# One step of a hybrid decoder layer on one core: 1 / rms of the input made during the second FFN pair, low parts of weights a step behind their casts, SSM sums a sample behind updates

## The chip, the cores and the metric

The kernel runs on one core of one Trainium2 chip. A core has a matrix engine (TensorE, PE in the profile, with its weight loads as PEld), three engines for elementwise work (VectorE = DVE, ScalarE = ACT, GpSimd = POOL) and SyncE (SP), which issues the DMAs. Each engine takes its own instructions in order; semaphores join them. The metric is the device time of one execution in microseconds (us), the median over the runs.

## The reference, cut to what matters

T = 1048 tokens (16 meta, 1024 of a prompt, 8 samples of one token each) go through one layer in f32, D = 1024, D_FF = 2816:

```python
def rmsnorm(x, w):
    y = x * lax.rsqrt(jnp.mean(x * x, axis=-1, keepdims=True) + EPS)
    return y * w

def swiglu(x, wg, wu, wd):
    return (jax.nn.silu(x @ wg) * (x @ wu)) @ wd

h += 0.5 * swiglu(rmsnorm(h))               # FFN 1
u  = rmsnorm(h) @ w_in                      # q, f, v, g of 4 HGRN2 heads; z, x, B, C, dt of Mamba-2
...                                         # HGRN2: f = lb + (1 - lb) sigmoid(u_f), k = 1 - f, q = silu(u_q)
...                                         # Mamba-2: conv + silu, chunked scan; per sample:
                                            #   state = exp(dt A) state + dt x B^T, y = state C + D x
h += concat(hgrn_out, ssm_out) @ w_out      # ssm_out = grouped rmsnorm(y * silu(z))
h += 0.5 * swiglu(rmsnorm(h))               # FFN 2
```

Outputs are the normed h and the states of both recurrences.

## The kernel before, in words

**Products.** A number in f32 is split into a high part, rounded to the type that TensorE multiplies (`CAST` on ACT), and a low part, the rest (a subtraction on DVE). A product takes three matmuls (`mm3`, L143 to L145: high × high, high × low, low × high).

**The FFN's pairs.** Gate and up projections of one block f of 128 columns (22 in all) are a *pair*. It is computed as a two by two block product in seven products (numbered 1 to 7) over two halves of the tokens: 14 *steps* of 12 matmuls. Each step's operands are blocks or sums of blocks: on the side of the tokens (class `Blocks`, named `o` and `e` in `first1` for the two halves, L287 sums, L292 high, L298 low parts, each 128 × 1048), on the side of the weights (class `Left`: loads, L360 sums, L364 high, L368 low parts, 128 × 512). After a step `post` adds the product into the results on DVE (`L452`, `L457`, `L462` and so on) or copies it on ACT (L450), multiplies by 1 / rms of the tokens (`times_r`, L445; the norm's weight is in the input blocks already) and applies silu. Two such pairs make the input of one block pair of the down projection (`Hidden.jobs`), which comes in its own 7 products.

**Order.** In both FFNs the order on PE, DVE, ACT and SP is written by hand: `S.add` appends a step, `S.before(i, fn)` puts work ahead of step i, and `Steps.run` issues all of it, on each engine in that order. In the middle of the kernel (projections, scans, output projection) a scheduler orders the instructions by the code and its own estimates.

**The head of FFN 1** (`first1`, classes `Input` and `Blocks`). x is loaded in ten tiles of 128 tokens and transposed on TensorE (`place`, L843; `place_k`, L868). Tiles 0 to 4 are the half `o`, tiles 5 to 9 the half `e`. Each transposed block is written scaled by the norm's weight (L855, L870) and raw (L859, L871; the raw blocks go to memory by `store`, to be added to h later). The sum of squares of each token is an ACT instruction per tile (`square`, L887). `rms(half)` makes 1 / rms of five tiles and writes it on the diagonal of identity tiles (L902), `spread_r(half)` multiplies these by ones so that each partition has the row (L908), and copies it (L909). In the first pair this was made for the half `o` ahead of step 5 and for `e` ahead of step 10, between the pair's own steps; the first pair's steps take the tokens half by half, the later pairs' by turns.

**The SSM scan.** `ssm_scan` takes nine chunks of 128 tokens: L1111 makes decays from running sums loaded from memory (`cumd`), L1112 an Exp, L1114 products on DVE, which TensorE needs at L1118; L1125 and L1129 update the state that TensorE needs in the next chunk (L1104). `ssm_samples` gives nine jobs, one for each of the 8 samples and one at the end, which are handed out in `hgrn_project` of the first head while the scan runs: a sample's state and B, C rows are loaded into two of the eight `r` buffers, POOL updates the state (L1191, L1195, L1196, per group g of heads), DVE sums it against C (four instructions, L1198), and SP stores it.

**The projections of HGRN2 head 0** (`hgrn_project`): for q a Silu (ACT) of each of three chunks of tokens, for f two Sigmoids (one for f and one for k = 1 − f), between the Exps of the scan. ACT loads a table (`ACT_TABLE_LOAD`) when the function changes.

**The second norm of Mamba-2** (`ssm_norm(K, 1, "u")`, L1232 to L1242): squares on ACT, a sum on POOL (L1233), three matmuls with ones (L1237), then a multiplication on DVE. After it comes `out_proj`.

Of the kernel before, what the change touches and what calls it, by code (L numbers as in the profile page):

```python
# [17 lines left out]
P = 128  # L18
# [5 lines left out]
NS = 8  # L24
# [318 lines left out]
class Left:  # L343
# [30 lines left out]
    def plan(self, S, s0, late):  # L374
# [52 lines left out]
def pair(K, S, wg, wu, f, ops, spread, hid, first=None):  # L427
# [20 lines left out]
    def post(p, cs, b):  # L448
        if p == 1:
            nc.scalar.copy(temp("z", cs), b)  # L450
        elif p == 6:
            nc.vector.tensor_add(temp("v", cs), b, temp("z", cs))  # L452
        elif p == 2:
# [4 lines left out]
        elif p == 7:  # L458
            nc.vector.tensor_add(temp("u1", cs), b, temp("x", cs))
            times_r("u1", 1, cs)  # L460
        elif p == 3:
            nc.vector.tensor_add(temp("g1", cs), b, temp("v", cs))  # L462
            t = times_r("g1", 1, cs)
            nc.scalar.activation(t, t, AF.Silu)  # L464
        else:
            nc.vector.tensor_add(temp("u0", cs), b, temp("v", cs))
            times_r("u0", 0, cs)
            if "h" not in tm:
                tm["h"] = True
                hid.append(K.slot("s", T))  # L470
            for n in range(2):
                nc.vector.tensor_mul(halves(hid[0][:, n * 2 * Q : n * 2 * Q + 2 * Q])[:, cs], temp(f"g{n}", cs), temp(f"u{n}", cs))

    if not first:
        left.plan(S, s0, int(f == 1))
# [5 lines left out]
    def post_first(p, cs, b):  # L481

        if p in (5, 2):
            late[p] = b
        elif p == 7:
            nc.vector.tensor_add(temp("u1", cs), b, temp("x", cs))
        elif p == 3:
            post(2, cs, late[2])
            post(3, cs, b)
            times_r("u1", 1, cs)  # L490
# [187 lines left out]
def ffn(K, wg, wu, wd, ops, spread, src, first, after):  # L678
# [9 lines left out]
    with K.tc.manual_schedule(engines={E.PE, E.DVE, E.Activation, E.SP}):  # L688
        S = Steps()
        hidden = Hidden(K)  # L690
        for i in range(NF // 2):
            hid, e = [], []
            for f in (2 * i, 2 * i + 1):
                hid.append([])
                pair(K, S, wgv, wuv, f, ops, spread, hid[-1], first if f == 0 else None)
                e.append(len(S.steps))
            hidden.jobs(S, i, hid, *e)
# [110 lines left out]
class Input:  # L808
# [3 lines left out]
    def __init__(self, K, a, wcol, ops, spread):  # L812
# [3 lines left out]
        self.x, self.diag = {}, {}  # L816
# [72 lines left out]
    def store(self, half):  # L889
        dv = self.d.rearrange("(b k p) t -> b p k t", p=P, b=2)  # L890
        for q in (2 * half, 2 * half + 1):
            for b in range(2):
                self.K.nc.sync.dma_start(dv[b][:, :, q * Q : q * Q + Q], self.raw[b, q])

    def rms(self, half):

        K = self.K
        token_rstd(K, *(self.st[:, j, 5 * half : 5 * half + 5] for j in range(3)))
        d = self.diag[half] = K.t(2 * Q)
        for i in range(5):  # L900
            c = slice(P * i, min(P * i + P, 2 * Q))
# [956 lines left out]
```

## Time and profile before

| | us |
|---|---|
| median of 3 runs | 2137.22 (2134.08 to 2138.86) |
| profiled execution, its own time | 2141.21 |
| its span | 2139.4 |
| TensorE busy | 2021.8 (95%) |
| VectorE busy | 1491.7 (70%) |
| ScalarE busy | 803.0 (38%) |
| GpSimd busy | 141.3 (7%) |

The span runs from the first to the last instruction of the profiled execution; 1.8 us of its time lie around it. FFN 1 begins at once and its pairs last until about 490 us, the scan is between 880 and 980, the second FFN's pairs lie between 1440 and 1860. A busy TensorE isn't always at its peak: the granted clock (PEclk) says at what share of full speed it ran. An engine's idle time matters only where TensorE waits for it. In rows of a timeline the columns are start, duration, engine, line, operation, output<-inputs, shape, count, and in brackets the idle time before and what ended it; DVE's sums of the samples stand there as CUSTOM_DVE_ANT_0, in the order below as ISA.

### The profile page before, as it was taken

Reading aid. Unit: us, or ns where it says so; the run is one execution under the profiler, and the core shown is the slowest. Engines: PE = TensorE matmul, PEld = TensorE weight load, DVE = VectorE, ACT = ScalarE, POOL = GpSimd, SP = SyncE. Lnnn points to the kernel's source line nnn. Section 1 sums busy time; section 2 is a strip of 40 time slices with the busy share of each in tenths; the row PEclk is TensorE's granted clock in tenths of the full one; section 3 lists DMA queues with packets and bytes.
Section 4 is the critical chain, followed back from the end, with each engine's and each line's share of the span. In section 5 each row is a group of like instructions: output and inputs, shape, how many; then the busy total and the mean of one; then the engine's idle time right before and its main releaser. Section 6 shows DMA issues by size and latency. Waiting matters only on the chain.

```text
span 2139.4 us, 38417 instructions
## 1 busy us (share of the span) xinstructions
PE 2021.8 (95%) x15495; PEld 1965.4 (92%) x15495; DVE 1491.7 (70%) x2489; ACT 803.0 (38%) x1494; POOL 141.3 (7%) x175
## 2 busy tenths in 40 slices
PE   5999999999899899799999998979999999989996
PEld 5999999999899889788989997979999999989996
DVE  6777777777787676596454366677777777778863
ACT  7422222223335443562432335652222222324342
POOL 1000000000002110321111010220000000000000
PEclk8999999999999999999999999999999999999999
DMA  6323333246956511452022053313233242587651
GB/s 189 89 81 100 103 93 105 78 131 228 295 165 194 155 47 31 119 154 75 32 71 79 2 176 107 103 60 106 88 107 105 76 120 81 172 265 230 208 166 59
DMA packets 325033, 259.17 MB, mean 121 GB/s; under 512 B 17712, under 2 KB 301104, under 8 KB 324848
## 3 DMA queue, kind: packets, MB, share of 16 engines
q1 hardware_dynamic: 324616, 256.68, 39.5%
q8 instruction: 122, 2.00, 0.4%
q14 instruction: 55, 0.45, 0.1%
q0 software_dynamic: 224, 0.04, 0.0%
q10 hardware_dynamic: 16, 0.00, 0.0%
HBM read 191.26 MB, written 65.47 MB: 120 GB/s over the span
## 4 chain that ended last, share of the span: by engine, by line
PE 78%; DVE 8%; DMA 6%; ACT 3%; issue 2%; SPq 1%; POOL 1%; DVEq 0%; ACTq 0%; POOLq 0%
PE acc L143 24%; PE acc L144 23%; PE acc L145 23%; DMA r<-in_w_ffn_down_dram 2%; DMA r<-in_w_ffn_up_dram 2%; PE mis L1355 2%; DMA u<-hd 1%; DVE s L634 1%; DVE u L287 1%; DVE r L360 1%; PE mis L1394 0%; PE mis L1450 0%; DVE ws L616 0%; DVE u L298 0%; PE mis L1412 0%
## 5 line engine op out<-in xcount | busy, mean ns | idle before, releaser
L143 PE MATMUL acc<-u,ws 128*128 128x262 f32 (+2 forms) x4504 | 1326.9, 296 | 56.5 <-DVE s L634 20.1
L144 PE MATMUL acc<-u,ws 128*128 128x262 f32 (+2 forms) x4504 | 1315.6, 292 | 0.6 <-DVE u L563 0.3
L145 PE MATMUL acc<-u,ws 128*128 128x262 f32 (+2 forms) x4504 | 1313.9, 292 | 1.0 <-DVE ws L368 0.8
L143 PEld LDWEIGHTS acc<-u,ws 128*128 128x128 f32 x4504 | 858.2, 191 | 75.1 <-issue 21.7
L144 PEld LDWEIGHTS acc<-u,ws 128*128 128x128 f32 x4504 | 862.4, 191 | 2.5 <-DVE u L563 0.7
L145 PEld LDWEIGHTS acc<-u,ws 128*128 128x128 f32 x4504 | 858.3, 191 | 1.9 <-DVE ws L368 1.0
L368 DVE TENSOR_TENSOR ws<-r,ws 128x512 fp32r<-128x512 f32 x308 | 212.0, 688 | 103.7 <-ACT ws L364 103.7
L364 ACT CAST ws<-r 128x512 fp32r<-128x512 f32 x308 | 173.3, 615 | 4.7 <-PE acc L145 3.1
L464 ACT ACTIVATE t<-t 128x524 f32<-128x524 f32 (+1 forms) x46 | 28.6, 622 | 313.1 <-DVE t L445 313.1
L360 DVE TENSOR_TENSOR r<-r,r 128x512 f32<-128x512 f32 x176 | 119.1, 697 | 19.0 <-DMA r<-in_w_ffn_up_dram 17.0
L634 DVE SCALAR_TENSOR_TENSOR s<-acc,s 128x524 f32<-128x524 f32 (+1 forms) x120 | 77.6, 663 | 48.8 <-PE acc L145 47.6
L455 ACT ACTIVATE t<-t 128x524 f32<-128x524 f32 (+1 forms) x46 | 28.7, 623 | 216.7 <-DVE t L445 216.7
L204 POOL TENSOR_TENSOR t<-t,t 128x262 f32<-128x262 f32 x56 | 52.9, 960 | 813.2 <-ACT t L203 813.2
L563 DVE TENSOR_TENSOR u<-u,u 128x1048 fp32r<-128x1048 f32 (+1 forms) x84 | 97.1, 1159 | 8.8 <-ACT u L559 8.8
L445 DVE TENSOR_TENSOR t<-t,u 128x524 f32<-128x524 f32 (+1 forms) x138 | 93.6, 681 | 4.7
L138 DVE TENSOR_TENSOR ws<-r,ws 128x512 fp32r<-128x512 f32 x88 | 60.2, 698 | 39.2 <-ACT ws L137 39.0
L611 ACT CAST ws<-r 128x512 fp32r<-128x512 f32 (+1 forms) x84 | 47.8, 581 | 102.9 <-DVE r L606 39.3
L616 DVE TENSOR_TENSOR ws<-r,ws 128x512 fp32r<-128x512 f32 (+1 forms) x84 | 57.2, 691 | 41.6 <-ACT ws L611 41.5
L611 ACT CAST ws<-u 128x512 fp32r<-128x512 f32 (+1 forms) x72 | 42.1, 585 | 113.2 <-DVE u L606 110.9
L559 ACT CAST u<-u 128x1048 fp32r<-128x1048 f32 (+1 forms) x84 | 83.2, 992 | 2.0 <-DMA u<-hd 2.0
L137 ACT CAST ws<-r 128x512 fp32r<-128x512 f32 x88 | 53.8, 617 | 71.7 <-PE acc L145 51.9
L445 DVE TENSOR_TENSOR t<-acc,u 128x524 f32<-128x524 f32 (+1 forms) x46 | 31.3, 680 | 61.6 <-PE acc L145 61.6
(379 smaller groups left out, 1950.1 us busy)
## 6 DMA issues: line engine op xcount, KB each, us to landing
hd<-s SPq DMA_DIRECT2D x170, 262.0 KB
r<-in_w_ffn_down_dram SPq DMA_DIRECT2D x128, 256.0 KB
u<-hd SPq DMA_DIRECT2D x56, 524.0 KB
r<-in_w_ffn_gate_dram SPq DMA_DIRECT2D x88, 256.0 KB
r<-in_w_ffn_up_dram SPq DMA_DIRECT2D x88, 256.0 KB
r<-in_w_in_dram SPq DMA_DIRECT2D x56, 256.0 KB
r<-in_w_ffn_down_dram SPq DMA_DIRECT2D x64, 192.0 KB
u<-hd SPq DMA_DIRECT2D x28, 393.0 KB
```

The source lines that it names most:

```text
L138: self.nc.vector.tensor_sub(lo, src, hi.bitcast(F32))
L143: mm(ps, whi, xhi, start=first, stop=False, skip_group_check=more)
L144: mm(ps, whi, xlo, start=False, stop=False, skip_group_check=more)
L145: mm(ps, wlo, xhi, start=False, stop=last, skip_group_check=more)
L360: self.K.nc.vector.tensor_tensor(self.raw[p], self.raw[x], self.raw[y], op)
L364: self.K.nc.scalar.copy(self.w[p][:, : self.n * P], self.raw[p])
L368: self.K.nc.vector.tensor_sub(t[:, 512 : 512 + w], self.raw[p], t[:, :w].bitcast(F32))
L445: nc.vector.tensor_mul(t, t if src is None else src, spread.lanes(i, cs))
L559: K.nc.scalar.copy(hi, lo.bitcast(F32))
L563: K.nc.vector.tensor_sub(lo, lo.bitcast(F32), hi.bitcast(F32))
L611: nc.scalar.copy(w[p, j, g][:, : n * P], src)
L634: nc.vector.scalar_tensor_tensor(t, b, 0.5, t, ALU.mult, ALU.add)
```

## The change

1. *The head.* All ten squares come later (two of the smaller tiles at steps 1 and 4, the others ahead of steps 9 to 16), `rms` is made once for all ten columns ahead of step 18, its diagonal is one buffer of full width, and the four spread matmuls stand ahead of step 22, in the second pair. The first pair's results stay unscaled until then: six jobs ahead of steps 26 to 31 do its scaling, silu and products. `post` of product 2 is an ACT copy in the first two pairs. The jobs of the first block pair of the down projection wait for that (steps 32 and 33), and the second pair's weight sums come four steps later. The first pair's other preparations are spread anew over steps 1 to 11.
2. *Weights.* In all pairs of both FFNs the loads come one step earlier, and the low part (L368) one step behind its cast. `times_r("u1")` goes from the post of product 7 to that of product 3.
3. *The samples.* Job b updates sample b on POOL and then sums sample b − 1 on DVE and stores it: ten jobs, four in place of three for each projection of head 0.
4. *Head 0's q and f.* ACT copies the chunks raw; Silu or the Sigmoids run once over all tokens, behind the third chunk.
5. *The second norm's end* (matmuls and multiplication) is written behind the first quarter of `out_proj`.

```diff
 class Left.plan
-            ((1, 7, 4, 2), (-10, -10, -9, -9), self.load),
-            ((5, 6, 7, 3), (-7, -7, -6, -5), self.sum_),
-            (ORDER, [2 * i - 4 + late for i in range(7)], self.split),
+            ((1, 7, 4, 2), (-11, -11, -10, -10), self.load),
+            ((5, 6, 7, 3), [d + sums for d in (-7, -7, -6, -5)], self.sum_),
+            (ORDER, [2 * i - 4 + late for i in range(7)], self.hi),
+            (ORDER, [2 * i - 3 + late for i in range(7)], self.lo),
 pair, post
+        elif p == 2 and late_r and f < 2:
+            nc.scalar.copy(temp("g0", cs), b)
 ...
         elif p == 7:
             nc.vector.tensor_add(temp("u1", cs), b, temp("x", cs))
-            times_r("u1", 1, cs)
         elif p == 3:
             nc.vector.tensor_add(temp("g1", cs), b, temp("v", cs))
-            t = times_r("g1", 1, cs)
-            nc.scalar.activation(t, t, AF.Silu)
+            if late_r and f == 0:
+                return
+            if late_r and f == 1:
+                silu(0, cs)
+            silu(1, cs)
+            times_r("u1", 1, cs)
 ...
+    if late_r:
+        cs = slice(0, 2)
+        for i, (fn, *args) in enumerate(((silu, 0, cs), (silu, 1, cs), (times_r, "u0", 0, cs), (product_, 0, cs), (times_r, "u1", 1, cs), (product_, 1, cs))):
+            S.before(s0 + late_r + i, lambda fn=fn, args=args: fn(*args))
 first1
-        before(S, 4, (o.low, 3), (w.lo, 3), (tail,), (e.cast, 1), (e.sum_, 5), (o.cast, 4), (x.place_k, 4), (x.rms, 0), (x.place_k, 5))
-        before(S, 5, (x.spread_r, 0), (o.low, 4), (e.cast, 5), (e.low, 1), (x.place_k, 6), (x.place_k, 7), (x.store, 1))
 ...
+        for i, n in enumerate((3, 5, 6, 7, 8)):
+            before(S, 12 + i, (x.square, n))
+        before(S, 18, (x.rms,))
+        before(S, 22, *((x.spread_r, q) for q in range(4)))
 ssm_samples
-            for j in (2 * g, 2 * g + 1):
-                nc.vector.tensor_tensor_reduce(up[:, j % 2], sb[:, j], rows[:, 2 + g], 1.0, 0.0, ALU.mult, ALU.add, ys[:, j, b : b + 1])
+    def sample(b):
+        if b < NS:
+            update(b)
+        if b > 0:
+            output(b - 1)
 hgrn_project
+            nc.scalar.copy(out[x][:, c0 : c0 + w], ps)
+            left[0] -= 1
+            if left[0] == 0:
+                (ev_q if x == "q" else ev_f)(0, T, out[x])
 out_proj
+        if u == 1 and mid:
+            mid()
```

What this does to the order of instructions at three places. First ACT in the head, from the cast of token block 5 on. Before (u and ws are operands of tokens and weights, L859 raw copies, L887 a square, L450 the copy of the first product):

```order
L292 CAST u_244<-u_241 128x1048
L364 CAST ws_248<-r_246 128x512
L859 COPY u_202<-mis_226 128x4x12
L859 COPY u_205<-mis_226 128x4x12
L887 ACTIVATE s_115,st_103<-s_115 128x1024
L450 COPY t_275<-acc_262 128x262
L292 CAST u_280<-u_259 128x1048
```

and now (L452 is the copy of the first product, L877 the raw copies, L888 and L889 a placement of the half e, L905 a square of a small tile):

```order
L452 COPY t_257<-acc_244 128x262
L292 CAST u_259<-u_242 128x1048
L364 CAST ws_263<-r_261 128x512
L877 COPY u_202<-mis_226 128x4x12
L877 COPY u_205<-mis_226 128x4x12
L905 ACTIVATE u_126,st_103<-u_126 12x1024
L888 ACTIVATE u_282<-mis_277,col_100 128x262
L889 COPY u_284<-mis_277 128x262
```

The cast of block 5 now stands behind the copy of the first product, the first placement of e ahead of the second step, and the square of a full tile is gone from here.

Second DVE in the scan, at the fourth chunk. Before (L1114 the chunk's products, L1198 the sums of sample 3, whose state is r_10418, L1125 what the scan goes on with):

```order
L1114 TENSOR_TENSOR s_9710<-s_9710,s_9712 128x512 x2
L1198 ISA t_10423,s_9643<-r_10418,r_10419 128x128
L1198 ISA s_9643 128x1
L1198 ISA t_10423,s_9643<-r_10418,r_10419 128x128
L1198 ISA s_9643 128x1
L1198 ISA t_10428,s_9643<-r_10418,r_10419 128x128
L1198 ISA s_9643 128x1
L1198 ISA t_10428,s_9643<-r_10418,r_10419 128x128
L1198 ISA s_9643 128x1
L1125 TENSOR_TENSOR s_9712<-mis_9751,s_9712 128x512
```

and now (L1130 and L1141 are those lines, L1221 the sums, of sample 2, whose state is r_10288):

```order
L1130 TENSOR_TENSOR s_9697<-s_9697,s_9699 128x512 x2
L1221 ISA t_10316,s_9630<-r_10288,r_10289 128x128
L1221 ISA s_9630 128x1
L1221 ISA t_10316,s_9630<-r_10288,r_10289 128x128
L1221 ISA s_9630 128x1
L1221 ISA t_10316,s_9630<-r_10288,r_10289 128x128
L1221 ISA s_9630 128x1
L1221 ISA t_10316,s_9630<-r_10288,r_10289 128x128
L1221 ISA s_9630 128x1
L1141 TENSOR_TENSOR s_9699<-mis_9738,s_9699 128x512
```

As many sums stand between the two lines, but those of the sample before.

Third PE at the second norm. Before (L1237 the norm's matmuls, L143 to L145 the projections; acc_13185 is the last of the gate's in its first rows, then the first of `out_proj`):

```order
L145 MATMUL acc_13185<-u_8294,ws_13045 128x348
L1237 MATMUL mis_13266<-u_13261,ones_83 128x350
L1237 MATMUL mis_13269<-u_13261,ones_83 128x350
L1237 MATMUL mis_13272<-u_13261,ones_83 128x348
L143 MATMUL acc_13185<-u_8287,ws_13303 128x262
```

and now (L1270 for L1237):

```order
L145 MATMUL acc_13176<-u_8281,ws_13036 128x348
L1270 MATMUL mis_13337<-u_13252,ones_83 128x350
L143 MATMUL acc_13176<-u_8274,ws_13275 128x262
L1270 MATMUL mis_13340<-u_13252,ones_83 128x350
L1270 MATMUL mis_13343<-u_13252,ones_83 128x348
L144 MATMUL acc_13176<-u_8282,ws_13275 128x262
```

The scheduler has put the norm's first matmul ahead of the projection still, and one matmul of it between.

More of the change, by code (lines that the diff above doesn't have):

```diff
@@ L694, in ffn @@
                 hid.append([])
-                pair(K, S, wgv, wuv, f, ops, spread, hid[-1], first if f == 0 else None)
+                pair(K, S, wgv, wuv, f, ops, spread, hid[-1], first if f == 0 else None, late_r)
                 e.append(len(S.steps))
-            hidden.jobs(S, i, hid, *e)
+            hidden.jobs(S, i, hid, *([late_r + 6, late_r + 7] if late_r and i == 0 else e))
         h = []
@@ L1614, in first1 @@
         o.low(2)
+        w.lo(2)
         o.sum_(5)
[L1616 to L1625 removed]
         def tail():
```

127 lines of the change are left out of this document (69 added, 58 removed).

## The prediction

> **What bounds the kernel now.** I read the page first (busy time, slices, chain), then TensorE's waits, and then windows and single instructions where TensorE isn't full.
>
> ```profile
> span 2139.4 us, 38417 instructions
> PE 2021.8 (95%) x15495; PEld 1965.4 (92%) x15495; DVE 1491.7 (70%) x2489; ACT 803.0 (38%) x1494; POOL 141.3 (7%) x175
> PE   5999999999899899799999998979999999989996
> PE 78%; DVE 8%; DMA 6%; ACT 3%; issue 2%; SPq 1%; POOL 1%; DVEq 0%; ACTq 0%; POOLq 0%
> ```
>
> TensorE bounds it, 95% busy, and the chain of waits is 78% TensorE. No edit removes matmuls in number, so the change can only win where TensorE stands still or runs at a low clock: the first slice, and the slices around 900 us. The first 100 us in four windows (columns: length, busy time and count of each engine, granted clock, DMA share, GB/s):
>
> ```profile
> core 0: us, PE busy (x) PEld busy (x) DVE busy (x) ACT busy (x) POOL busy (x), PEclk, DMA share, GB/s
> 25.00:50.00 25.00, 17.98 (x104) 16.26 (x102) 14.54 (x27) 22.78 (x58) 0.00 (x0) 0.75 0.23 63
> 50.00:75.00 25.00, 18.12 (x108) 17.46 (x108) 21.61 (x39) 18.95 (x35) 0.00 (x0) 0.80 0.25 74
> 75.00:100.00 25.00, 25.00 (x207) 25.00 (x206) 18.57 (x31) 7.13 (x13) 0.00 (x0) 1.00 0.31 94
> ```
>
> From 75 us on TensorE is full: 207 matmuls in 25 us, 0.121 us each, so a step of the pair (12 matmuls) takes 1.45 us. Before that it does 104 and 108, at clocks of 0.75 and 0.80.
>
> **Part 1, the head of FFN 1: −7.5 us.** The first pair's 14 steps, as TensorE saw them:
>
> ```profile
> 21.97 0.58 PE L143 MATMUL acc<-u,ws 128*128 128x262 f32 x1 [4.13 <-ACT t L450]
> 42.78 2.12 PE L908 MATMUL mis<-t,ones 128*128 128x262 f32 x4 [4.81 <-ACT t L902]
> 55.19 0.59 PE L143 MATMUL acc<-u,ws 128*128 128x262 f32 x1 [5.12 <-ACT t L450]
> 64.33 1.73 PE L908 MATMUL mis<-t,ones 128*128 128x262 f32 x4 [1.75 <-ACT t L902]
> 72.75 0.28 PE L143 MATMUL acc<-u,ws 128*128 128x262 f32 x1
> ```
>
> The second step (step 1) starts at 21.97, the second pair at 72.75: 50.8 us for 13 steps, which at 1.45 would take 18.9. That leaves 32 us, of which the spread of 1 / rms shows 4.81 + 1.75 of waiting and 2.12 + 1.73 of slow matmuls. What ACT and DVE have to make for these steps is priced by these groups (0 to 75 us; columns: busy us, mean ns, idle before):
>
> ```profile
> L292 ACT CAST u<-u 128x1048 fp32r<-128x1048 f32 x14 | 14.8, 1068 | 2.1 <-DVE u L287 2.1
> L887 ACT ACTIVATE s<-s 128x1024 f32<-128x1024 f32 x8 | 8.6, 1078 | 0.0
> L870 ACT ACTIVATE u<-mis,col 128x262 f32<-128x262 f32 (+1 forms) x16 | 8.1, 506 | 0.0
> L871 ACT COPY u<-mis 128x262 f32<-128x262 f32 (+1 forms) x16 | 6.4, 399 | 0.0
> L298 DVE TENSOR_TENSOR u<-u,u 128x1048 fp32r<-128x1048 f32 x14 | 17.2, 1243 | 0.4 <-ACT u L292 0.4
> L287 DVE TENSOR_TENSOR u<-u,u 128x1048 f32<-128x1048 f32 x8 | 10.0, 1244 | 0.0
> L368 DVE TENSOR_TENSOR ws<-r,ws 128x512 fp32r<-128x512 f32 x9 | 6.2, 685 | 0.0
> L360 DVE TENSOR_TENSOR r<-r,r 128x512 f32<-128x512 f32 x8 | 5.4, 686 | 0.0
> ```
>
> Moved off the first pair's way: 8 squares (8.6 us of ACT), the 10 pieces of the diagonal, the spread and its waits, the scaling and silu. What must still be made there: on DVE 12 low parts at 1.24, 8 sums at 1.24, 9 weight pieces at 0.69, with eight adds of the products at 0.43 (estimate, half of a full-width add): 14.9 + 9.9 + 6.2 + 3.4 = 34.5 us; on ACT 12 casts at 1.07, 16 + 16 placements at 0.51 and 0.40, and some 5 of weight casts and copies: 12.8 + 14.5 + 5 = 32.3. Both begin near 18 us, so the last step can't begin before about 52: at most 20 us can come back. The beginning can't be earlier either:
>
> ```profile
> GB/s 0 61 135 292 297 284 371 338 348 329 203 282 321 362 404 406 422 387 355 346 336 277 331 328 200 222 229 200 73 3 0 0 0 0 0 154 342 49 0 0
> 12.29 1.06 PE L843 MATMUL mis<-ident,s 128*128 128x128 f32 x8 [1.22 <-DMA s<-in_x_prompt_dram]
> 18.00:20.00 2.00, 0.00 (x0) 0.00 (x0) 2.00 (x5) 1.28 (x2) 0.00 (x0) 0.50 1.06 351
> 22.00:24.00 2.00, 2.00 (x9) 2.00 (x10) 2.00 (x4) 1.44 (x3) 0.00 (x0) 0.50 1.04 330
> ```
>
> Summing the first row (1 us slices), the tile that TensorE takes at 12.29 was through at about 9.7 us, and all of x with the weights between (5.29 MB) is through at 18.1. With the same lag the last tile is usable at 20.5, and step 1 now stands behind its first placement: about 21.4 against 21.97, no gain. From there I walked ACT and DVE through the new order, an instruction starting when its engine and its inputs are free (each hand-off costs what the row gives): step 1 ends at 24.1, steps 3, 5 and 7 at 30.1, 38.3 and about 50.2, the last two low parts are written at 57.4 and 59.6, and the last step ends near 61.7. Against 72.75 that is −11. From it goes back: the four spread matmuls now lie in the full second pair (in before 2.12 + 1.73 = 3.85, half of that at full clock, +1.9, nothing else covers them), and the first pair's scaling, silu and products land in steps 25 to 38, where DVE gets some 31 instructions of about 0.65 in 14 steps of 1.45: 20.2 against 20.3 us, no slack, so +1.6 for two or three of them that come late (2.5 × 0.65). Sum −7.5; from −3 (the walk's hand-offs hold at half of its gain) to −11.
>
> The trace shows 18 to 20 at a clock of 0.50, and 22 to 24 too (9 matmuls in 2.00, 0.22 each), behind a wait of 4.13; in the new order TensorE stands from 21.97 − 4.13 = 17.84 to the placement at 20.5, 2.7. The Trainium skill, TensorE: Matmul & The Clock Gate, section HAM oscillation, has the clock drop after some 3.4 us of idleness. By that rule 12 matmuls after 2.7 would keep the full clock, an estimated 1.2 us less; no row here shows a wait of 2.7, and I leave it out.
>
> **Part 2, low parts a step behind, loads a step earlier, one scaling moved: −1 us.** What stands there, in the full pairs of FFN 1 (75 to 490 us; columns: total, times, longest):
>
> ```profile
> PE acc L143 <- DVE t L457: 1.4, 4, 0.5
> DVE ws L368 <- ACT ws L364: 49.0, 41, 1.2
> ```
>
> DVE waits 49 us for casts, but TensorE only 1.4 in all for it: DVE's idleness costs nothing, so 1.4 in each FFN is the most to be had, and a low part written later can cost as much where DVE is late: −1, from −2 to +1.5.
>
> **Part 3, the SSM scan, sums a sample behind updates, Silu and Sigmoid late: −7 us.** Two waits of TensorE, and the windows around them:
>
> ```profile
> PE mis L1118 <- DVE s L1114: 7.6, 2, 6.2
> PE mis L1104 <- DVE s L1125: 5.6, 2, 5.2
> 892.42 2.44 ACT L1111 ACTIVATE s<-s,s 128x128 f32<-128x128 f32 x8 [3.92 <-DMA s<-cumd]
> 894.88 1.28 ACT L1121 ACT_TABLE_LOAD   x1
> 898.60:904.80 6.20, 6.18 (x32) 5.25 (x32) 0.48 (x1) 6.08 (x11) 1.38 (x2) 0.53 0.99 268
> 904.80:910.00 5.20, 0.09 (x1) 0.00 (x0) 3.67 (x9) 0.00 (x0) 5.20 (x9) 0.80 0.27 75
> 910.00:915.00 5.00, 4.91 (x20) 4.91 (x20) 5.00 (x13) 3.30 (x6) 1.75 (x3) 0.53 0.55 124
> 906.33 0.80 DVE L1198 CUSTOM_DVE_ANT_0 t<-r,r 128x128 f32<-128x128 f32 x1 [7.26 <-POOL r L1196]
> ```
>
> The second wait (5.2) is an order on DVE: what the scan waits for (L1125) is queued behind the sums of sample 3, and these wait 7.26 for POOL. In the new order sample 2's stand there, whose update ended earlier, so the 5.2 goes, with the slow clock after it: 910 to 915 runs at 0.53, half of 4.6 us is 2.1. The first wait (6.2) is for cumd, whose load stays behind a store on SP; only the table load of 1.28 goes, since the raw copies leave Exp's table in place. 5.2 + 2.1 + 1.3 = 8.6. Against it: SP's load of sample 6 waits for a buffer freed behind chunk 3, with chunk 4's cumd queued behind it, which nothing covers; I take off a fifth for it, 1.6, and at worst all 8.6 goes back. −7, from 0 to −12 (two more of the waits behind POOL gone).
>
> **Part 4, the end of the second norm put behind the first projection: 0.**
>
> ```profile
> PE mis L1237 <- POOL u L1233: 4.7, 1, 4.7
> ```
>
> In TensorE's new order the first of the norm's three matmuls still stands ahead of the projection's first, and one matmul of that between it and the others, so the 4.7 stays (at best −0.1; at worst +0.5, if the multiplications by the norm come late).
>
> **Sum.** −7.5 − 1 − 7 = −15.5. The profiled execution took 2141.21 (span 2139.4 and 1.8 around it), 3.99 above the median of the runs: 2125.7 for it, 2121.7 for the median; I say 2122.
>
> **The rivals.**
> *The head is bound by hand-offs and not by work* (14%). For: DVE was busy 14.54 of 25 and still late. Then the walk's gain shrinks to 3.5, which the spread and the jam mostly take: −2 instead of −7.5, 2127.
> *The scan waits elsewhere* (13%). For: the loads on SP. Its second wait then becomes one of cumd, −0 for −7: 2129.
> *More than I count* (12%): the head −11, the scan −12, the pairs −2: 2112.
> *Nothing gained* (9%): both of the first two together leave −2 − 1 − 0 = −3, 2134; with the pairs' +1.5 in place of −1 about 2137.
> *Slower* (6%): sums beside updates. The prices of one sum, and of L1129 beside POOL and later:
>
> ```profile
> L1198 DVE CUSTOM_DVE_ANT_0 t<-r,r x32: 277/286/1134, 886.9 to 946.6; 128x128 f32<-128x128 f32 x32
> L1198 DVE CUSTOM_DVE_ANT_0 t<-r,r 128x128 f32<-128x128 f32 x32 | 14.5, 501 | 9.1 <-POOL r L1196 9.1
> 922.37 2.96 DVE L1129 SCALAR_TENSOR_TENSOR u<-u,s,s 128x128 f32<-128x128 f32 x4
> 933.08 1.13 DVE L1129 SCALAR_TENSOR_TENSOR u<-u,s,s 128x128 f32<-128x128 f32 x4
> ```
>
> A sum takes 0.28 alone and 0.80 to 1.13 beside POOL (shortest, median and longest in the first row). At a mean of 0.50 (second row) some 8 of 32 lie beside it now: 24 × 0.28 + 8 × 1.13 = 15.8, about the 14.5 there. If the 24 others come to lie beside the next sample's update too, that is 24 × 0.85 = 20.4, and four chunks' L1129 at 2.96 for 1.13 add 7.3: 27.7 us of DVE within the scan. If TensorE waits for all of it, the scan is 27.7 − 8.6 = +19.1, the total −7.5 − 1 + 19.1 = +10.6, 2148. It decides where the surplus exceeds 8.6 + 8.5 = 17 us; against it, DVE did nothing in most of 898.60 to 904.80 (0.48 of 6.20), so there is slack. The Trainium skill, SBUF — State Buffer, section Who interferes with whom, says that a VectorE instruction with two SBUF inputs and a GpSimd one that reads SBUF block each other wholly; the 0.80 beside the 0.28 agrees in direction.
>
> **How the numbers follow.** The forecast has 46%. A measurement of this kernel tells about 0.2% (4.3 us) from no change. Faster by more than that: forecast, both half-failures, the larger gain: 85%. Within: 9%. Slower: 6%. The range leaves out the last two and the far end of the larger gain: 2111 (head −11, pairs −2, scan −12, less 1) to 2133 (half of the head alone).
>
> **What would show it.** Right: the second pair starts near 63 us in place of 72.75; no wait at L1104 of 5 us near 905; the wait at the second norm stays near 4.7; 75 to 490 unchanged within 2 us but for some 3 lost in the second pair. Wrong: the second pair at 70 or later; sums (L1221 after) of 0.8 or more with TensorE waiting behind them; more than 5 us of waits between 65 and 90.

## The result and the profile after

The changed kernel takes 2120.10 us, median of 5 runs (2118.52 to 2124.35), against 2138.86 for the kernel before (5 runs, 2134.08 to 2144.28): ratio 0.9915, 95% interval 0.9895 to 0.9934, so 18 us less (14 to 22). The forecast was 2122, 15.5 less. The profiled execution took 2120.27, its span is 2118.6; that of before was 2139.4.

The head of FFN 1, in the windows of 25 us that were shown of before (same columns):

```profile
25.00:50.00 25.00, 15.67 (x100) 13.59 (x99) 18.60 (x23) 18.49 (x44) 0.00 (x0) 0.87 0.46 135
50.00:75.00 25.00, 23.38 (x177) 22.28 (x177) 17.55 (x31) 20.84 (x45) 0.00 (x0) 0.99 0.15 43
```

From 50 to 75 us TensorE does 177 matmuls instead of 108. From 25 to 50 it does no more than before; it stands for 9 us there (7 before), but the granted clock is 0.87 (0.75 before). TensorE's timeline at the points that the forecast named:

```profile
20.20 0.57 PE L143 MATMUL acc<-u,ws 128*128 128x262 f32 x1
45.06 0.59 PE L143 MATMUL acc<-u,ws 128*128 128x262 f32 x1 [3.57 <-ACT u L292]
60.47 0.29 PE L143 MATMUL acc<-u,ws 128*128 128x262 f32 x1
72.64 1.93 PE L924 MATMUL mis<-u,ones 128*128 128x262 f32 x8
74.22 0.48 PE L143 MATMUL acc<-u,ws 128*128 128x262 f32 x1
```

Step 1 starts at 20.20 (21.97 before) and the second pair at 60.47 (72.75). What lies between them took 40.3 us in place of 50.8. The one long wait that is left is for a cast of token block 2 of e ahead of step 7. The spread of 1 / rms stands in the second pair, and the next product starts 74.22 − 72.64 = 1.58 us later for it.

The waits of TensorE in the scan and at the second norm (columns: total, times, longest; L1134 and L1120 are L1118 and L1104 of before, L1270 is L1237):

```profile
PE mis L1134 <- DVE s L1130: 4.8, 3, 3.1
PE mis L1120 <- DVE s L1141: 0.2, 1, 0.2
PE mis L1270 <- POOL u L1261: 4.7, 1, 4.7
```

The wait of 6.2 is half as long, that of 5.2 is gone, and the one at the norm is as it was. What was said of the second of these lines ahead of the prediction is wrong: L1125 and L1129 (now L1141 and L1145) make the chunk's output, and it is L1137 and L1138 that update the state. L1104 takes nothing from either; it transposes B into a PSUM tile. By the source (not shown by a run) it waits there until L1125 has read one of the four such tiles, which is then used again. The sums of the samples (mean 501 ns before):

```profile
L1221 DVE CUSTOM_DVE_ANT_0 t<-r,r 128x128 f32<-128x128 f32 x32 | 14.0, 484 | 0.0
```

They have not become dearer.

To place the differences I read six points from the traces of all kernels and took the stages between them, in us. *Head*: from step 1 to the second pair. *Pairs 1*: from there to the first sum of the down projection. *Scan*: from the first decays (L1111) to the last square of the second norm (the scan, the HGRN2 heads and the gates; work moves over the borders within, so it isn't cut further). *Pairs 2*: in FFN 2, from the first sum of the first pair to the first sum of the down projection. The ratio is to the kernel before, which was run again beside each group of experiments (medians 2135.95 to 2140.03), with its 95% interval.

| kernel | step 1 at | head | pairs 1 | scan | pairs 2 | ratio |
|---|---|---|---|---|---|---|
| before | 21.97 | 50.8 | 444.8 | 419.5 | 461.0 | |
| changed | 20.20 | 40.3 | 446.7 | 407.4 | 460.5 | 0.9915 (0.9895–0.9934) |
| head alone | 19.59 | 40.4 | 448.5 | 421.0 | 464.4 | 0.9980 (0.9965–0.9994) |
| sums alone | 20.67 | 50.8 | 445.4 | 413.2 | 464.0 | 0.9994 (0.9982–1.0006) |
| raw copies alone | 21.49 | 50.8 | 444.9 | 413.7 | 462.5 | 0.9986 (0.9976–0.9995) |
| weights' plan alone | 20.48 | 49.3 | 443.0 | 416.4 | 461.1 | 0.9984 (0.9970–0.9998) |
| changed, sums twice | 19.91 | 40.4 | 445.2 | 420.7 | 459.9 | 0.9971 (0.9956–0.9985) |
| changed, sums undone | 19.59 | 40.2 | 444.8 | 413.6 | 461.1 | 0.9929 (0.9907–0.9951) |
| changed, step 7 first | 19.88 | 43.6 | 445.2 | 408.1 | 459.9 | 0.9929 (0.9913–0.9945) |
| that, norm's sum on VectorE | 20.10 | 41.6 | 446.6 | 413.8 | 459.3 | 0.9916 (0.9901–0.9932) |
| changed, sums of e on GpSimd | 19.15 | 42.8 | 444.6 | 413.2 | 459.7 | 0.9935 (0.9916–0.9954) |
| changed, plan undone | 20.34 | 41.4 | 448.6 | 414.1 | 464.5 | 0.9965 (0.9950–0.9980) |
| changed, lows undone | 20.34 | 40.5 | 445.8 | 414.7 | 459.8 | 0.9925 (0.9906–0.9944) |
| changed, loads undone | 19.04 | 40.1 | 447.4 | 410.8 | 461.6 | 0.9948 (0.9930–0.9967) |

Each row is one execution. Where the code of a stage is the same, the rows show its scatter: 0.1 to 1.3 us in the head, 1 to 3.5 in the pairs, 3.5 us either way in the scan. So a stage says what a change does there sooner than the time of the whole kernel, whose runs scatter over 10 us.

### The profile page after: what moved, and what is told of

It reads as the page before. It is cut to its first block, busy times and chain, and to the rows that moved or that the text cites. A ratio compares the mean times of both kernels' runs of the same rounds, so it can differ in the third digit from the quotient of the medians.

```text
span 2118.6 us, 38401 instructions
## 1 busy us (share of the span) xinstructions
PE 2012.7 (95%) x15495; PEld 1956.1 (92%) x15495; DVE 1490.9 (70%) x2473; ACT 800.4 (38%) x1490; POOL 141.5 (7%) x175
## 3 DMA queue, kind: packets, MB, share of 16 engines
q1 hardware_dynamic: 324616, 256.68, 40.2%
## 4 chain that ended last, share of the span: by engine, by line
PE 79%; DVE 9%; DMA 5%; ACT 3%; issue 2%; SPq 1%; POOL 0%; DVEq 0%; ACTq 0%; POOLq 0%
PE acc L143 24%; PE acc L145 24%; PE acc L144 24%; PE mis L1401 1%; DMA r<-in_w_ffn_down_dram 1%; DMA r<-in_w_ffn_up_dram 1%; DMA u<-hd 1%; DMA s<-in_x_prompt_dram 1%; DVE s L652 1%; DMA s<-cumd 1%; DVE t L447 1%; DVE u L287 1%; DVE ws L368 1%; DVE u L298 0%; DVE s L1415 0%
## 5 line engine op out<-in xcount | busy, mean ns | idle before, releaser
L143 PE MATMUL acc<-u,ws 128*128 128x262 f32 (+2 forms) x4504 | 1328.3, 296 | 49.5 <-DVE s L652 20.8
L145 PE MATMUL acc<-u,ws 128*128 128x262 f32 (+2 forms) x4504 | 1315.4, 292 | 3.3 <-DVE ws L368 3.2
L143 PEld LDWEIGHTS acc<-u,ws 128*128 128x128 f32 x4504 | 858.1, 191 | 66.8 <-issue 21.4
L145 PEld LDWEIGHTS acc<-u,ws 128*128 128x128 f32 x4504 | 858.5, 191 | 5.6 <-DVE ws L368 4.5
L368 DVE TENSOR_TENSOR ws<-r,ws 128x512 fp32r<-128x512 f32 x308 | 212.0, 689 | 78.3 <-ACT ws L364 78.1
L360 DVE TENSOR_TENSOR r<-r,r 128x512 f32<-128x512 f32 x176 | 122.1, 697 | 12.7 <-DMA r<-in_w_ffn_up_dram 10.8
L138 DVE TENSOR_TENSOR ws<-r,ws 128x512 fp32r<-128x512 f32 x88 | 60.3, 700 | 40.2 <-ACT ws L137 40.0
L137 ACT CAST ws<-r 128x512 fp32r<-128x512 f32 x88 | 53.6, 617 | 66.5 <-PE acc L145 47.6
L452 ACT COPY t<-acc 128x524 f32<-128x524 f32 (+1 forms) x46 | 26.6, 579 | 112.2 <-PE acc L145 112.2
```

Of the source, the lines that this page charges most:

```text
L138: self.nc.vector.tensor_sub(lo, src, hi.bitcast(F32))
L143: mm(ps, whi, xhi, start=first, stop=False, skip_group_check=more)
L145: mm(ps, wlo, xhi, start=False, stop=last, skip_group_check=more)
L360: self.K.nc.vector.tensor_tensor(self.raw[p], self.raw[x], self.raw[y], op)
L368: self.K.nc.vector.tensor_sub(t[:, 512 : 512 + w], self.raw[p], t[:, :w].bitcast(F32))
```

## The experiments

**1. The head alone.** The changed kernel with everything else taken back (plan of the weights, scaling of u1, samples, q and f, norm).

```diff
-            (ORDER, [2 * i - 4 + late for i in range(7)], self.hi),
-            (ORDER, [2 * i - 3 + late for i in range(7)], self.lo),
+            (ORDER, [2 * i - 4 + late for i in range(7)], self.split),
...
-        evs.update(q=ev_raw("q"), f=ev_raw("f"))
...
-    return [lambda b=b: sample(b) for b in range(NS + 1)] + [skip]
+    return [lambda b=b: sample(b) for b in range(NS)] + [skip]
```

> Only the head of the first FFN is changed (squares, one rms, spread in the second pair, first pair scaled behind it); the loads and low parts of the weights, the sums of the samples, q and f of head 0 and the second norm stay as before. My theory: the second pair begins near 60.5 us as in the changed kernel (before 72.75), some 2 us are given back until the down projection, and the time is 9 to 11 us below that of before (ratio 0.995 to 0.996), the scan keeping both waits (6.2 and 5.2). Rival, that the later low parts of the weights carry part of the gain in the pairs: the time is less than 7 us below before, and waits of TensorE for weights turn up between 60 and 490 us.

TensorE's timeline at the second pair, and then its waits in the scan:

```profile
59.95 0.29 PE L143 MATMUL acc<-u,ws 128*128 128x262 f32 x1
```

```profile
PE mis L1136 <- DVE s L1132: 6.7, 4, 4.8
PE mis L1122 <- DVE s L1143: 5.1, 2, 4.9
```

The second pair starts at 59.95, the scan keeps both waits (4.8 and 4.9): the head's gain belongs to this part alone, and the scan's to others. The rival is half right: the time fell by less than 7 us, but no wait of TensorE for weights turned up between 60 and 490 us. Pairs 1 took 448.5 instead of 444.8 to 445.4, so 3.5 is given back, not 2. The time fell by 4.3 us (1.3 to 7.5), less than the 9 to 11 that I expected; in FFN 2, which this kernel doesn't touch, its pairs took 464.4 where the profiled execution of before took 461.0. Experiments 10 and 11 come back to that.

**2. The sums alone**, and **3. the raw copies alone**, each put into the kernel before.

```diff
+    def sample(b):
+        if b < NS:
+            update(b)
+        if b > 0:
+            output(b - 1)
```

> Only the samples' jobs are changed: sample b is updated and sample b-1 summed, ten jobs, four for each projection of head 0. My theory: the wait of 5.2 us at the state's matmul near 905 us goes with the slow clock behind it, 5 to 8 us below before (ratio 0.996 to 0.9975), while the wait of 6.2 us at the chunk's products stays above 4. Rival, that the raw copies of q and f are what frees the scan: less than 3 us, and a wait of some 5 us stays.

```diff
+    if hd == 0:
+        evs.update(q=ev_raw("q"), f=ev_raw("f"))
```

> Only head 0's q and f are changed: raw copies by chunk and one Silu or pair of Sigmoids at the end. My theory: one table load of 1.28 us goes from the way of the Exp, the wait of 6.2 us becomes about 5, that of 5.2 us stays, 1 to 2 us below before (ratio 0.999 to 1.0). Rival: the copies themselves free ACT so that both waits shrink, 5 us or more below before.

TensorE's waits in the scan, with the sums alone:

```profile
PE mis L1118 <- DVE s L1114: 6.3, 4, 5.0
PE mis L1104 <- DVE s L1125: 2.7, 2, 2.3
```

and with the raw copies alone:

```profile
PE mis L1118 <- DVE s L1114: 6.5, 4, 3.3
...
PE mis L1104 <- DVE s L1125: 1.9, 2, 1.1
```

Each of the two parts shortens the wait of 5.2 (to 2.3 and 1.1), and the raw copies take most from the wait of 6.2 (3.3), too. Each makes the scan's stage some 6 us shorter (413.2 and 413.7 for 419.5; the two other kernels with the old scan took 416.4 and 421.0). My theory gave the raw copies only the table load. Why they do more stands on ACT and DVE. ACT with the raw copies alone, and behind it DVE (timelines):

```profile
889.53 2.46 ACT L1111 ACTIVATE s<-s,s 128x128 f32<-128x128 f32 x8 [2.34 <-DMA s<-cumd]
891.89 0.62 ACT L1121 ACTIVATE s<-s 128x512 f32<-128x512 f32 x1
895.69 0.44 ACT L1275 COPY u<-acc 128x348 f32<-128x348 f32 x1
896.02 1.07 ACT L1112 ACTIVATE s<-s 128x1024 f32<-128x1024 f32 x1
...
898.98 0.69 DVE L1125 TENSOR_TENSOR s<-mis,s 128x512 f32<-128x512 f32 x1 [4.06 <-PE mis L1124]
908.73 1.13 DVE L1198 CUSTOM_DVE_ANT_0 t<-r,r 128x128 f32<-128x128 f32 x1
```

From the first decays to the second Exp (L1112) there is a copy of 0.44 and no table load; before, three loads of 1.28 and a Silu stood there. The stretch takes 7.6 us (889.53 to 897.1) in place of 11.8 (892.42 to 904.2). The wait for cumd is 2.34 instead of 3.92. And the scheduler, with other work on ACT, now puts L1125 ahead of the sums, which come ten us later: the order on DVE that the forecast blamed is changed by this part as well. In time the two parts gave 1.3 us (−1.3 to 3.9), where I had expected 5 to 8, and 3.0 (1.1 to 5.1), where I had expected 1 to 2. One thing was not tried: in the kernel before, GpSimd began sample 3's update at 903.42, after 8.06 us of waiting for the load of that sample's state, so an earlier load might have shortened the wait of 5.2 as well.

**4. The plan of the weights alone**, in the kernel before (loads one step earlier, low parts one behind; u1 as before).

```diff
-            ((1, 7, 4, 2), (-10, -10, -9, -9), self.load),
+            ((1, 7, 4, 2), (-11, -11, -10, -10), self.load),
...
-            (ORDER, [2 * i - 4 + late for i in range(7)], self.split),
+            (ORDER, [2 * i - 4 + late for i in range(7)], self.hi),
+            (ORDER, [2 * i - 3 + late for i in range(7)], self.lo),
```

> Only the plan of the weights is changed in all pairs but the first: loads one step earlier, low parts one step behind their casts. My theory: DVE's waits for casts (49 us in the first FFN's pairs) shrink to under 10, TensorE's waits there by about 1 us for each FFN, and the time is within 2.5 us of before (ratio 0.999 to 1.0005). Rival, that DVE's waiting costs TensorE time that the waits do not show: 5 us or more below before.

DVE's waits in the pairs of FFN 2 (1440 to 1840 us), here

```profile
DVE ws L368 <- ACT ws L364: 46.3, 38, 1.2
...
DVE r L360 <- DMA r<-in_w_ffn_up_dram: 5.8, 8, 1.5
```

and in the kernel before:

```profile
DVE ws L368 <- ACT ws L364: 46.7, 39, 1.3
...
DVE r L360 <- DMA r<-in_w_ffn_up_dram: 7.3, 10, 1.3
```

The first half of my theory fell: DVE waits for casts as long as before. The time was 3.4 us less (0.4 to 6.4), beyond the 2.5 that I had allowed, and head and pairs 1 together 3.3.

**5. The sums twice**, the test of the slower case.

```diff
-        for j in range(4):
+        for j in (0, 1, 2, 3, 0, 1, 2, 3):
             nc.vector.tensor_tensor_reduce(junk[:, j], sb[:, j], rows[:, 2 + j // 2], 1.0, 0.0, ALU.mult, ALU.add, ys[:, j, b : b + 1])
```

> The changed kernel with each of the 32 sums of the samples made twice (the second writes the same numbers again). My theory: VectorE has slack in the scan, so 32 more sums of 0.28 to 0.8 us (9 to 25 us of VectorE) lengthen the scan by less than 5 us; the time is within 5 us of the changed kernel (ratio to before 0.990 to 0.995). Rival, the slower case of the prediction: the sums lie on TensorE's way beside GpSimd, and at least 10 us of them appear as waits: ratio 0.996 or more.

TensorE's waits in the scan, and the group of the sums on DVE:

```profile
PE mis L1134 <- DVE s L1130: 10.4, 5, 4.2
PE mis L1120 <- DVE s L1141: 2.9, 1, 2.9
```

```profile
L1221 DVE CUSTOM_DVE_ANT_0 t<-r,r 128x128 f32<-128x128 f32 x64 | 23.2, 417 | 0.0
```

The rival is right about the slack. The sums take 23.2 us for 14.0, 9.2 more (the short instructions that read them out lie nearly all within the next sum); TensorE's waits in the scan grow by 8.3 (10.4 + 2.9 for 4.8 + 0.2), the stage by 13.3, and the ratio is 0.9971 for 0.9915, some 12 us (5 to 19 by the ends of the two intervals). DVE has next to no slack in the scan: some 9 us of more work there cost at least about as much in time. The slower case didn't come because its other premise was wrong, that the sums would come to lie beside the next sample's update. A sum beside an update is still dear in the changed kernel (up to 1.14 us, 0.28 the shortest), but the mean of 484 ns for 501 says that no more of them lie there than before.

**6. The sums undone**, in the changed kernel.

> The changed kernel, but each sample is summed directly behind its own update, nine jobs, three for each projection of head 0, as before. My theory now: the raw copies already took most of both waits (alone they made the scan 3.6 us shorter, the sums alone 5.0, both 7.7), so the scan is about 4 us longer than in the changed kernel, 104 us from the first decays to the first product of head 0's scan, and the time 2 to 5 us above it (ratio to before 0.992 to 0.994). Rival, the prediction's own account: the wait of 5.2 us stands again behind the sums, and the scan is 6 us longer or more.

```profile
PE mis L1134 <- DVE s L1130: 8.5, 4, 4.9
...
PE mis L1120 <- DVE s L1141: 0.2, 1, 0.2
```

The wait of 5.2 does not come back, so this part of the rival fell; another, of 4.9 for 3.1, grows at the chunk's products. The scan took 413.6 for 407.4, but the seven kernels that have both parts lie between 407.4 and 414.7. The ratio 0.9929 is above 0.9915 by 3 us, with intervals that overlap widely (from −6 to +12). Whether the sums give anything on top of the raw copies is not settled.

**7. Step 7 first.** Another order on ACT against the wait of 3.57 that is left in the head.

```diff
-        before(S, 6, (e.low, 1), (e.cast, 5), (o.cast, 4), (x.place_k, 5), (x.place_k, 6))
-        before(S, 7, (x.place_k, 7), (e.cast, 2), (e.low, 5), (e.low, 2), (e.sum_, 6), (x.store, 1, (1,)))
-        before(S, 8, (e.cast, 6), (o.low, 4), (e.sum_, 7), (e.low, 6), (e.cast, 7))
+        before(S, 6, (e.low, 1), (x.place_k, 5, False), (x.place_k, 6, False))
+        before(S, 7, (x.place_k, 7, False), (e.cast, 2), (x.raw_k, 5), (e.low, 2), (e.cast, 5), (e.low, 5), (e.sum_, 6), (x.raw_k, 6), (x.raw_k, 7), (x.store, 1, (1,)))
+        before(S, 8, (e.cast, 6), (o.cast, 4), (o.low, 4), (e.sum_, 7), (e.low, 6), (e.cast, 7))
```

> The changed kernel with another order on ACT ahead of steps 6 to 8 only: the raw copies of the last three placements and the casts of blocks 5 (e) and 4 (o) come behind the cast of block 2 (e), which step 7 waits for. My theory: ACT's order and not its amount of work makes that wait (3.57 us, with half a clock for 5 us behind it); step 7 starts some 4 us earlier, the second pair at 56 to 58 us in place of 60.5, and the time is 2 to 5 us below the changed kernel (ratio to before 0.989 to 0.991). Rival: ACT and DVE are bound by their work until the last low part, so later steps wait instead: the second pair starts within 1 us of 60.5, no change in time.

```profile
43.96 0.39 PE L143 MATMUL acc<-u,ws 128*128 128x262 f32 x1 [1.88 <-ACT u L292]
53.83 0.59 PE L144 MATMUL acc<-u,ws 128*128 128x262 f32 x1 [3.88 <-DVE u L298]
```

Step 7 starts 1.1 us earlier and waits 1.88 instead of 3.57, and step 9 waits 3.88 for a low part that cost it 0.57 in the changed kernel. The second pair starts at 63.46, 3 us later than there, and the ratio, 0.9929, shows no gain. The rival is right that the wait only moves, though not for its reason: ACT and DVE both stand still in between (ACT here):

```profile
47.86 0.38 ACT L456 COPY t<-acc 128x262 f32<-128x262 f32 x1 [1.35 <-PE acc L145]
48.14 2.03 ACT L292 CAST u<-u 128x1048 fp32r<-128x1048 f32 x2
52.69 2.03 ACT L292 CAST u<-u 128x1048 fp32r<-128x1048 f32 x2 [2.52 <-issue]
```

The cast for step 9 stands behind a copy of step 7's product, so ACT waits for TensorE while TensorE will wait for ACT. The head is set by hand-offs between three engines.

**8. The same, with the norm's sum on VectorE** instead of GpSimd.

```diff
-    K.nc.gpsimd.tensor_add(v, v, r)
+    (K.nc.vector if g else K.nc.gpsimd).tensor_add(v, v, r)
```

> As the kernel with step 7 first, and the sum of squares of the second norm is added on VectorE in place of GpSimd. My theory: the wait of 4.7 us at the norm's first matmul falls by 1 to 2 us (GpSimd takes 2.41 us for this sum, VectorE 1.2 for one of that size), the rest as there: 1 to 2 us below it, ratio to before 0.988 to 0.991. Rival: VectorE is late there by its low parts of weights, the wait stays at 4 us or more, no change against the kernel with step 7 first.

```profile
PE mis L1277 <- DVE u L1268: 3.6, 1, 3.6
```

The wait at the norm falls by 1.1 (4.7 to 3.6), as expected. In the whole kernel, 0.9916 against 0.9929 and 0.9915, that can't be seen. By the ratio, no version that I ran beats the changed kernel.

**9. Three sums of e on GpSimd**, in the changed kernel.

```diff
-        self.K.nc.vector.tensor_sub(t, x, y)
+        eng = self.K.nc.gpsimd if self.half and self.first and p != 5 else self.K.nc.vector
+        eng.tensor_sub(t, x, y)
```

> The changed kernel with three sums of token blocks of the half e (6, 7 and 4; each 128 x 1048, 1.24 us on VectorE) made on GpSimd, which stands idle in the first pair. My theory: what sets the head now is the chain cast, low part, matmul and sum, not VectorE's amount of work; a sum on GpSimd takes about 2.4 us (as its sum of this size at the second norm), so each link that holds one gets longer: the second pair starts 1 to 4 us later than 60.5, the time is 0 to 4 us above the changed kernel (ratio to before 0.991 to 0.9935). Rival: VectorE's 3.7 us less work is what counts, the second pair starts 2 us earlier or more.

GpSimd (POOL) and DVE between 42 and 50 us; the first row is all three sums together, the others are single sums and low parts:

```profile
42.67 9.19 POOL L290 TENSOR_TENSOR u<-u,u 128x1048 f32<-128x1048 f32 x3 [31.32 <-ACT u L891]
42.67 2.40 POOL L290 TENSOR_TENSOR u<-u,u 128x1048 f32<-128x1048 f32 x1 [31.32 <-ACT u L891]
43.84 2.33 DVE L301 TENSOR_TENSOR u<-u,u 128x1048 fp32r<-128x1048 f32 x1 [4.50 <-ACT u L295]
45.02 3.43 POOL L290 TENSOR_TENSOR u<-u,u 128x1048 f32<-128x1048 f32 x1
46.09 3.47 DVE L301 TENSOR_TENSOR u<-u,u 128x1048 fp32r<-128x1048 f32 x1
```

The three sums take 3.06 each on the mean, and the first two low parts of DVE beside them 2.33 and 3.47 in place of 1.24: 3.7 us of work were taken from DVE, and 3.3 came back in these two alone. The second pair started at 61.91, 1.4 us later, as expected; the head took 42.8 for 40.3. The first sum, which GpSimd began before DVE, took 2.40, as alone. Each low part began beside a running sum and ended some 1.1 us after it (46.17 for 45.07, 49.56 for 48.45), as if its own work began only then; and the second sum, begun beside a low part, ended 2.3 us after that one. The Trainium skill, SBUF — State Buffer, section Who interferes with whom, has a VectorE instruction with two SBUF inputs contend with a GpSimd one that reads SBUF, for a port that one of them holds alone; these rows agree with it.

**10. The plan undone**, in the changed kernel (with the scaling of u1), and **11. half of it each**: the low parts back to their casts; the loads back by a step.

> The changed kernel with the weights' plan of before in all pairs (loads, low parts directly behind their casts, the scaling of u1 behind product 7). My theory: the plan gives about 2 us between the second pair and the first sum of the down projection in the first FFN (446.7 us in the changed kernel) and nothing in the second; the time is 1 to 3 us above the changed kernel, ratio to before 0.992 to 0.993. Rival: with the head's work moved into the second and third pair the plan is needed there, and TensorE waits 5 us or more for weights and sums between 60 and 120 us.

> The changed kernel with each low part of the weights directly behind its cast again; the loads stay one step earlier and the scaling of u1 behind product 3. My theory now: the plan's gain comes from the loads (VectorE's waits for the up weights in the second FFN's pairs are 7 to 12 us with the loads of before and 3 to 6 with the early ones), so the second FFN's pairs stay at 459 to 461 us as in the changed kernel (463 on average with the plan of before), and the time is within 2 us of it, ratio to before 0.990 to 0.9925. Rival: the low parts carry it, the pairs are back at 463 or more, ratio 0.993 or more.

> The changed kernel with the loads of the weights as late as before; the low parts stay a step behind their casts and the scaling of u1 behind product 3. My theory: VectorE's waits for the up weights in the second FFN's pairs go up from 4 to 7 us or more, the pairs from 460 to 462 us or more, ratio to before 0.9925 or more. Rival: pairs at 459 to 461 and the time as in the changed kernel, the loads give nothing.

DVE's waits in the pairs of FFN 2 (1440 to 1840 us), for casts and for the up weights, with the plan undone,

```profile
DVE ws L368 <- ACT ws L364: 47.6, 39, 1.3
...
DVE r L360 <- DMA r<-in_w_ffn_up_dram: 8.2, 9, 2.1
```

with the lows undone,

```profile
DVE r L360 <- DMA r<-in_w_ffn_up_dram: 4.9, 6, 1.6
```

and with the loads undone:

```profile
DVE ws L368 <- ACT ws L364: 35.2, 39, 1.2
...
DVE r L360 <- DMA r<-in_w_ffn_up_dram: 7.7, 11, 2.1
```

TensorE waits there three times for a sum on DVE with the plan undone (2.6 us in all, 1420 to 1850), and here is one of these waits, first on DVE, then on TensorE:

```profile
1673.92 1.42 DVE L360 TENSOR_TENSOR r<-r,r 128x512 f32<-128x512 f32 x2 [2.06 <-DMA r<-in_w_ffn_up_dram]
1675.25 0.70 DVE L460 TENSOR_TENSOR t<-acc,t 128x524 f32<-128x524 f32 x1
```

```profile
1676.10 0.36 PE L143 MATMUL acc<-u,ws 128*128 128x262 f32 x1 [1.04 <-DVE t L460]
```

The plan is worth more than I gave it: undoing it costs 10.7 us in time (0.9965 for 0.9915; from 3 to 18 by the ends of the two intervals), 2 us in pairs 1 and 4 in pairs 2. My rival for it, 5 us or more of waits between 60 and 120 us, did not come: they are 0.8 in all. The loads carry the larger part of the time: with them late the ratio is 0.9948, 7 us above the changed kernel, and DVE waits 7.7 us for weights; with the low parts back it is 0.9925 and 4.9 us, as I had expected. The low parts a step behind give nothing that can be seen. The rows show how a late load reaches TensorE: a weight sum (L360) that waits 2.06 us for its load holds up the sum of a product (L460) behind it on DVE, and TensorE waits 1.04 for that one.

The loads are not all of it. With them late, pairs 2 take 461.6, and 464.5 with all three parts undone; the two kernels differ by the low parts and by the scaling of u1. That scaling can be seen on DVE: in the eight kernels of which it is a part, DVE waits 34.6 to 35.2 us for casts in these pairs, in the six others 46.3 to 47.6, wherever loads and low parts stand. So it is this move that shortens the waits which I had expected the low parts to shorten in experiment 4. What it is worth to TensorE stays open; it wasn't tried by itself. Nor is it settled why the plan gives 3.4 alone and 10.7 when taken away: the intervals overlap, and the plan alone left u1 where it was.

## Why the prediction held, step by step

- **The beginning of step 1**: no gain was forecast (21.4 for 21.97). The ten kernels with the new head start it between 19.04 and 20.34, the four with the old one between 20.48 and 21.97: some 1.3 us. TensorE had waited there for the copy of the first product (L450), and on ACT that copy no longer stands behind a cast and a square.
- **The walk of the head**: 61.7 − 21.4 = 40.3 us from step 1 to the second pair. Measured 40.3, and 40.1 to 40.5 in five others with the same order there (41.4 in one). It holds on the way, too, and not only at the end. The walk had steps 1, 3, 5 and 7 end at 24.1, 30.1, 38.3 and 50.2, the last two low parts at 57.4 and 59.6, and the last step at 61.7; measured are 23.1, 29.1, 37.1 and 49.1, 56.1 and 58.2, and 60.5, each 1.0 to 1.4 earlier, as step 1 began 1.2 earlier. The account by instruction durations and hand-offs was right to a fraction of a us; the first rival of the forecast, that hand-offs would eat the gain, fell, although the head *is* bound by hand-offs (7, 9): the walk had counted them. The last two low parts on DVE:

```profile
54.82 1.24 DVE L298 TENSOR_TENSOR u<-u,u 128x1048 fp32r<-128x1048 f32 x1
...
56.92 1.24 DVE L298 TENSOR_TENSOR u<-u,u 128x1048 fp32r<-128x1048 f32 x1
```

- **What goes back in the second pair and behind it**: 1.9 + 1.6 = 3.5. Measured 3.5 (head alone, pairs 1, 448.5 against 445.0 on average), of it 1.58 for the spread; that the rest is the late scaling, as the prediction had it, wasn't followed up.
- **The plan**: −1 was the term that was mis-sized. In pairs 1 it gives 2 to 3 us and in pairs 2 some 3 (the five kernels without it: 461.0 to 464.5, mean 463.3; the seven with early loads and late low parts, six of them with u1's scaling moved as well: 459.3 to 461.1, mean 460.2). The step that failed read "1.4 in each FFN is the most to be had" from the waits of one execution. That execution was the best of its kind: with the same code, pairs 2 took 462.5 to 464.5 in four other kernels, with waits of 1.9 to 3.2 for DVE where before had 0.5. (A wait of 6.3 to 6.4 at the beginning of FFN 2's pairs, just ahead of the stage, is in every kernel, old and new; nothing here touches it.)
- **The scan**: −7. Measured 419.0 (mean of the three with the old scan) to 411.7 (mean of the seven with the new one), −7.3. The size was right, its account half, and that the two halves came to −7 is in part luck: the wait of 5.2 shrinks by either of the two parts (to 2.3 and 1.1), since the raw copies make the scheduler order DVE anew; and the raw copies take 3 us and not 1.3 from the wait of 6.2, with the wait for cumd 1.6 shorter. The 2.1 for the clock was not seen by itself (the changed kernel runs from 885 to 895 at 0.65 and 0.67); half of 4.6 is 2.3 and not 2.1, which changes nothing.
- **The second norm**: 0. The wait is 4.7 in both.
- **The sum**: head −10.4 − 1.3 + 3.5 = −8.2, plan −2.5 − 3.1 = −5.6, scan −7.3: −21 by stages, 20.8 between the two profiled spans, 18 (14 to 22) between the medians. The single parts' times add up to −12 (each ± 3); whether the 6 us to −18 are chance or a gain that only all of it together has, these runs don't tell. That 2122 came within 2 us of 2120.1 is thus in part luck: step 1's 1.3 and 4.6 of the plan were not in the forecast.

The clock: by the Trainium skill, TensorE: Matmul & The Clock Gate, section HAM oscillation, step 1 would have kept the full clock behind a wait under 3.4 us, a gain estimated at 1.2 us. I left it out, and rightly: in the changed kernel no wait of TensorE between 6.3 and 23 us is longer than 1.30, and step 1 runs at half the clock all the same. Its longest wait there, and then the windows:

```profile
11.86 1.06 PE L861 MATMUL mis<-ident,s 128*128 128x128 f32 x8 [1.30 <-DMA s<-in_x_prompt_dram]
```

```profile
10.00:12.00 2.00, 0.70 (x8) 0.50 (x6) 1.74 (x5) 2.00 (x4) 1.18 (x6) 1.00 1.14 274
12.00:14.00 2.00, 1.75 (x17) 1.44 (x16) 1.48 (x2) 2.00 (x6) 0.00 (x0) 1.00 1.10 364
14.00:16.00 2.00, 0.92 (x5) 0.56 (x5) 2.00 (x6) 2.00 (x4) 0.00 (x0) 1.00 1.02 408
16.00:18.00 2.00, 2.00 (x13) 1.94 (x11) 2.00 (x3) 0.30 (x2) 0.00 (x0) 0.53 1.03 404
20.00:22.00 2.00, 1.93 (x9) 1.93 (x10) 2.00 (x4) 2.00 (x7) 0.00 (x0) 0.50 0.88 276
```

The clock falls between 16 and 18 us, in a window in which TensorE is full; in two of the three windows ahead of it TensorE stood idle for more than half of the time, in pieces of at most 1.30. From 6.3 to 13.7 us TensorE did transposes only (L861). Whether the pieces of idleness or the kind of work made the clock fall is not shown.

## What to carry to other kernels

Where three engines hand work to each other, a walk through the new order with the durations and waits of the old trace gave the time to a fraction of a us here; moving a step forward in the same chain only moved the wait. A small wait in one execution is not the most that an edit can gain: compare the same stage over several executions or kernels before a term is set to nothing. Before work is moved to an idle GpSimd, look for two-input work of VectorE beside it, and before work is added to an engine that seems idle, double it there and see.

## What was not expected of the hardware

- Three sums of 128 × 1048 took 9.19 us on GpSimd instead of 7.2 (three times 2.40), and two low parts on VectorE beside them 5.73 instead of 2.4.
- The clock of TensorE fell to a half at about 16 us, though no single wait in the 9 us before was above 1.3 us; in 10 to 12 and 14 to 16 it was busy for 0.70 and 0.92 of 2.00; and after a wait of 3.57 it stayed there from 45.06 until about 50 us, with steps of 2.6 us in place of 1.45.
- Three table loads of 1.28 on ACT lay on the way of two Exps of the scan; with Exp's table kept the stretch is 4.2 us shorter (7.6 for 11.8).
